# A hybrid attention and state-space block: the mixer's TensorE order written out, loads moved ahead of two stages, and a tail with its residual tiles loaded ahead

## The chip, the cores and the metric

The kernel runs on one core of one Trainium2 chip. The time is the device time of one execution in microseconds (us). Of the kernel before, three runs took 2443.05, 2445.43 and 2448.56 us; the median is 2445.43. A core has TensorE (PE in the profile; PEld is its weight load), VectorE (DVE), ScalarE (ACT), GpSimd (POOL) and SyncE (SP), whose queue here starts nearly all DMA transfers. Instructions on one engine run in order; engines wait for each other by semaphores.

## The reference

One layer on x of 1024 positions by 1024 channels, cut here to what the change touches:

```python
h = rmsnorm(x, pre_norm_mix) * (1.0 + scale_m) + shift_m
proj = h @ w_in          # q_lat, kv_lat, k_idx, w_idx, z, xbc, dt_raw, g_a, g_b
y_a = sparse_mla_attention(...) @ w_o_attn
y_b = ssd_mixer(z, xbc, dt_raw, ...) @ w_o_ssd
mix = (sigmoid(g_a) * y_a + sigmoid(g_b) * y_b) @ w_out
x = x + gate_m * rmsnorm(mix, post_norm_mix)
h2 = rmsnorm(x, pre_norm_ffn) * (1.0 + scale_f) + shift_f
u_gate, u_up = split(h2 @ w_ffn_in, 2)
f = (silu(u_gate) * u_up) @ w_ffn_out
x = x + gate_f * rmsnorm(f, post_norm_ffn)
```

`ssd_mixer` is a Mamba-2 scan: 32 heads in 8 groups, a state carried from chunk to chunk, y = (C Bᵀ · decay) X inside a chunk plus C · state from the chunks before, then `rmsnorm(y * silu(z), ssd_norm)`. All is float32.

## The kernel before, in words

Activations lie with channels on the 128 partitions and positions along the free axis, in two halves of 512 positions (b = 0, 1). A float32 product is made of three matmuls in the fp32r format: each operand is split into a high part (ACT copy) and the rest (subtraction on DVE or POOL), and hi·hi, hi·lo and lo·hi are added in PSUM. Weights come through the stream `W`: SP loads a piece of 4 tiles (`wraw`), ACT makes `whi` (L147), POOL `wlo` (L148); two pieces are ahead of the one in use. TensorE then runs 12 matmuls on a piece for one half.

Stages in order of time: input norm and projections; attention; the **mixer**; the **merge**; the second sub-layer (`early`, `gate_up`, L1324); its output product (`pfo`, L1456) with the **tail**.

*Mixer* (about 1135 to 1490 us). 32 slices of the scan, one per chunk of 256 positions and group, group by group. A slice is `ssd_in` (loads; `pcb` = C Bᵀ, L1027; transposes `px`, L1038, and `pbn`, L1047; the decay masks M on ACT and DVE) and then, one slice later, `ssd_out` (`pyd` = M X, L1071 and L1072; the state's update `pst`, L1078; `pyo` = C · state, L1083; the sum, the gate z, and a store to `d_y`). Beside them runs a filler, `beside`: 8 column tiles of g_b (`pw`), then 8 of y_a = attention output @ w_o_attn (`poa`), each in steps of 6 matmuls. Between these two lies the loading and splitting of the attention output (`atl`, 16 tiles of 128x512). `weave` alternates the steps of `ssd_in`, `ssd_out` and the filler, but this only gives priorities: the instruction order of every engine, TensorE too, comes from a scheduler that simulates the program and picks what is ready. In other stages `in_order` ties TensorE to the program's order.

*Merge*. `y_load` brings the scan's output from `d_y` (`yl`), ACT makes `yh` (L1166) and DVE `yw` (L1167): 16 slices k of 128 channels for one half. `merge` multiplies them by w_o_ssd (`pos`, 48 matmuls for a column tile), `mixed` by w_out (`pot`). In the kernel before, `y_load(0, range(16))` stands behind the whole mixer in program order.

*Tail*. For the last column tile of half 1 the product is made in two pieces of 256 positions; `outputs` multiplies the scaled tile `fv` by the spread norm `prn` (DVE, L1474), adds the residual `x1l` that SP loads from `d_x1` there and then (L1473, L1475), and stores it (L1476).

Buffers: H (32 tiles of 128x512), Q (26), R (8 of 128x1024), EV (9 of 128x512 for passing data), 5 PSUM banks for the slices. A tile waits until a buffer of its kind is free.

## Time and profile before

| | us |
|---|---|
| median of three runs | 2445.43 |
| profiled execution | 2446.71, its span 2444.9 |
| TensorE busy | 2374.4 (97% of the span) |
| DVE, ACT, POOL busy | 1434.9, 1225.8, 1081.3 |
| mean granted TensorE clock | 0.985 |

"Granted clock" is the share of full speed at which TensorE may run; 0.50 is half. A stretch of time is given by its start and end in us from the span's start; what TensorE lost in it is the stretch less its busy time, and, where the clock is below 1.00, the stretch times the missing share.

### The profile page before, as it was taken

The numbers are of one execution on the slowest core, as the hardware profiler recorded it, in microseconds if no ns is written. First come the engines' busy times: TensorE is split into PE (matmuls) and PEld (weight loads), VectorE is DVE, ScalarE is ACT, GpSimd is POOL, SyncE is SP. The second block draws the span as 40 slices with busy tenths as digits, with TensorE's granted clock in tenths as the row PEclk, the third lists the DMA queues.
The fourth block names the chain that finished last, engine by engine and source line by source line (L and its number), as shares of the span: only waits on it lengthen the run. The fifth ranks groups of instructions, "written<-read, shape, count | busy, mean of one in ns | idle before, by whom it ended". The sixth has DMA issues, their size and how long they took to land.

```text
span 2444.9 us, 34790 instructions
## 1 busy us (share of the span) xinstructions
PE 2374.4 (97%) x11940; PEld 1938.1 (79%) x11940; DVE 1434.9 (59%) x2848; ACT 1225.8 (50%) x2351; POOL 1081.3 (44%) x877
## 2 busy tenths in 40 slices
PE   7999999999999999999999999999999999999997
PEld 5788888888888788887777767888777888888886
DVE  4566776599656666665567675456476666542211
ACT  4346665567446555556666564544453222344432
POOL 2731112222235545442345435557576545544564
PEclk8999999999999999999999999999999999999998
DMA  7224212522223232234768784655564544354453
GB/s 270 91 87 127 70 64 79 164 91 100 87 63 100 91 101 85 90 97 149 222 215 266 224 275 140 223 188 165 163 213 162 160 155 150 113 167 152 137 164 112
DMA packets 219745, 352.79 MB, mean 144 GB/s; under 512 B 22016, under 2 KB 86192, under 8 KB 219568
## 3 DMA queue, kind: packets, MB, share of 16 engines
q1 hardware_dynamic: 218848, 349.99, 44.3%
q8 instruction: 94, 1.54, 0.3%
q14 instruction: 83, 0.68, 0.1%
q10 hardware_dynamic: 720, 0.58, 0.1%
HBM read 266.31 MB, written 87.32 MB: 145 GB/s over the span
## 4 chain that ended last, share of the span: by engine, by line
PE 60%; DVE 4%; DMA 3%; ACT 2%; issue 2%; POOL 2%; SPq 0%; DVEq 0%; POOLq 0%; ACTq 0%
PE p L1324 14%; PE pfo L1456 9%; PE pw L232 8%; PE pos L222 5%; PE plg L774 4%; PE poa L232 3%; PE pot L222 3%; PE po L823 2%; PE pt L807 2%; PE puq L222 2%; PE pyd L1071 1%; PE pst L1078 1%; DMA a<-w_ffn_in 1%; PE pcb L1027 1%; PE pyo L1083 1%
## 5 line engine op out<-in xcount | busy, mean ns | idle before, releaser
L148 POOL TENSOR_TENSOR wlo<-wraw,whi 128x512 fp32r<-128x512 f32 x242 | 329.3, 1363 | 531.9 <-ACT whi L147 463.9
L1324 PE MATMUL p<-xh,wr 128*128 128x512 f32 x880 | 275.4, 392 | 3.7 <-DVE g L1374 3.7
L147 ACT ACTIVATE whi<-wraw 128x512 fp32r<-128x512 f32 x242 | 151.1, 627 | 207.7 <-issue 42.3
L1456 PE MATMUL pfo<-a,fwh 128*128 128x512 f32 (+1 forms) x684 | 208.7, 386 | 1.2 <-DVE a L243 1.2
L1318 POOL TENSOR_TENSOR wr<-a,wr 128x512 fp32r<-128x512 f32 x110 | 152.9, 1403 | 101.8 <-ACT wr L1317 65.9
L1324 PEld LDWEIGHTS p<-xh,wr 128*128 128x128 f32 x880 | 166.6, 189 | 39.0 <-DVE g L1374 4.1
L1324 PE MATMUL p<-xl,wr 128*128 128x512 f32 x440 | 172.2, 391 | 0.0
L243 POOL TENSOR_TENSOR fwl<-fw,fwh 128x512 fp32r<-128x512 f32 x92 | 113.9, 1241 | 116.0 <-ACT fwh L242 109.0
L1456 PEld LDWEIGHTS pfo<-a,fwh 128*128 128x128 f32 x684 | 127.5, 188 | 28.2 <-DVE a L243 2.6
L786 ACT ACTIVATE lg<-lg,mx 128x256 f32<-128x256 f32 (+7 forms) x128 | 98.9, 773 | 70.1 <-DVE mx L783 69.1
L1456 PE MATMUL pfo<-a,fwl 128*128 128x512 f32 (+1 forms) x342 | 131.9, 386 | 0.0
L1317 ACT ACTIVATE wr<-a 128x512 fp32r<-128x512 f32 x110 | 67.9, 629 | 123.9 <-PE p L1324 95.3
L313 POOL TENSOR_TENSOR adaw<-adaw,cs 128x512 f32<-128x512 f32 x64 | 66.7, 1044 | 133.4 <-DMA adaw<-ada_w 99.0
L242 ACT ACTIVATE fwh<-fw 128x512 fp32r<-128x512 f32 x92 | 54.5, 594 | 124.7 <-PE pfo L1456 102.8
L1324 PE MATMUL p<-h2h,wr 128*128 128x512 f32 x352 | 112.4, 396 | 0.0
L634 ACT ACTIVATE junk<-acc,cand__2203 128x1024 bf16<-128x1024 f32 (+2 forms) x96 | 86.2, 898 | 44.9 <-DVE cand__2203 L677 29.0
L222 PE MATMUL pos<-yw,whi 128*128 128x512 f32 x256 | 103.0, 402 | 4.8 <-DVE yw L1167 4.8
L222 PE MATMUL pos<-yh,whi 128*128 128x512 f32 x256 | 101.5, 397 | 3.9 <-ACT yh L1166 2.3
L222 PE MATMUL pos<-yh,wlo 128*128 128x512 f32 x256 | 102.1, 400 | 0.9 <-POOL wlo L148 0.9
L585 DVE SCALAR_TENSOR_TENSOR acc<-rel,widx,acc 128x384 f32<-128x384 f32 (+2 forms) x90 | 87.1, 987 | 25.0 <-ACT rel L580 24.8
L580 ACT ACTIVATE rel<-prel 128x512 f32<-128x512 f32 (+3 forms) x160 | 77.1, 523 | 48.7 <-PE prel L579 45.2
L1324 PEld LDWEIGHTS p<-xl,wr 128*128 128x128 f32 x440 | 83.3, 189 | 17.3
(572 smaller groups left out, 6864.0 us busy)
## 6 DMA issues: line engine op xcount, KB each, us to landing
wraw<-w_in SPq DMA_DIRECT2D x130, 256.0 KB, 2.9
a<-w_ffn_in SPq DMA_DIRECT2D x124, 256.0 KB, 3.3
fw<-w_ffn_out SPq DMA_DIRECT2D x80, 256.0 KB, 2.7
adaw<-ada_w SPq DMA_DIRECT2D x64, 256.0 KB, 3.0
al<-d_ac SPq DMA_DIRECT2D x32, 512.0 KB, 5.5
wraw<-w_o_ssd SPq DMA_DIRECT2D x64, 256.0 KB, 3.3
al<-d_a SPq DMA_DIRECT2D x44, 256.0 KB, 5.3
d_a<-g SPq DMA_DIRECT2D x40, 256.0 KB, 2.4
```

The source lines that it names most:

```text
L147: behind(S.activation(hi[:, :kt], raw[:, :kt], AF.Copy))
L148: behind(G.tensor_tensor(lo[:, :kt], raw[:, :kt], f(hi[:, :kt]), op=OP.subtract))
L222: T.matmul(o, wt[:, k0 + i, :], xs[k][xi][b][:, sl], start=pi == 0 and i == 0 and wt is hi and xi == 0, stop=pi == len(pcs) - 1 and i == l ...
L232: T.matmul(o, wt[:, k0 + j, :], xs[k][xi][b], start=i == 0, stop=i == 23)
L243: (lo_eng or V).tensor_tensor(lo, src, f(hi), op=OP.subtract)
L585: V.scalar_tensor_tensor(acc[i][:, 0:n], rel[:, 0:n], ws, acc[i][:, 0:n], op0=OP.mult, op1=OP.add)
L634: S.activation(jk, y, AF.Sign, scale=-1.0, bias=a_, accum_out=o)
L774: T.matmul(p[:, 0:w2], st[qi], KVT[ki][:, o_:o_ + w2], start=x == 0, stop=x == 2)
L786: S.activation(lg[:, 0:n], lg[:, 0:n], AF.Exp, scale=-1.0, bias=m, accum_out=rr[:, 2 * t + hh:2 * t + hh + 1])
L1318: G.tensor_tensor(w[:, 1], src, f(w[:, 0]), op=OP.subtract)
L1324: T.matmul(p, w[:, wi, i], X[x][i][xi], start=start and i == 0 and k == 0, stop=i == 3 and k == 2, skip_group_check=True)
L1456: T.matmul(p, w[wi][:, k - k0], xs[k][xi][:, sl], start=k == 0 and i == 0, stop=k == FT - 1 and i == 2)
```

## The change

Five things change. (1) The mixer's TensorE instructions are tied to the program's order, and the loop is written out: all four steps of `ssd_in`, then three of `ssd_out` (its `yield` between the two halves of `pyd` is gone), with 4 or 3 filler steps spread between them, by turns. (2) Four of the attention output's tiles of half 0 are loaded into Q before the last g_b tile; the others follow it. (3) The y_a tiles 0 to 4 are made for both halves, tiles 5 to 7 first for half 0 and then for half 1, with their weights loaded a second time. (4) `y_load(0, range(12))` stands before those last three tiles of half 1, in H and Q; the four other slices stay where they were. (5) In the second sub-layer's output the residual tiles of a whole half are loaded ahead into Q; the norm of the first 256 positions is applied after 8 of the 22 k-tiles instead of 12, and its additions go to DVE and POOL by turns.

```diff
@@ ssd_out
-            if j == 0:
-                yield
@@ beside
         for t in range(8):
+            if t == 7:
+                at_load(0, range(AT_IN_Q), Q)
             yield from gate_steps(57 + t, d_gb[t])
+        at_load(0, range(AT_IN_Q, KT), H_)
+        at_load(1, range(KT), H_)
+        for ts, bs in [((t,), BS) for t in range(POA_BOTH)] + [(range(POA_BOTH, 8), (b,)) for b in BS]:
+            for t in ts:
+                W.plan(col_tile(a["w_o_attn"][t]))
+                w = wpieces(ks8)
+                for b in bs:
...
+            if bs == (0,):
+                y_load(0, range(12), y_place)
@@ mixer
-    if True:
+    with in_order(mybir.EngineType.PE):
         prev = None
-        for s_ in [(c, g) for g in range(GROUPS) for c in range(NCH)] + [None]:
+        for n, s_ in enumerate([(c, g) for g in range(GROUPS) for c in range(NCH)] + [None]):
             z = {}
-            weave(ssd_in(*s_, z) if s_ else iter(()), 4 if s_ else 0, ssd_out(*prev) if prev else iter(()), 4 if prev else 0, filler, 4)
+            steps = ([ssd_in(*s_, z)] * 4 if s_ else []) + ([ssd_out(*prev)] * 3 if prev else [])
+            k, nf = 0, 4 - n % 2
+            for _ in range(0 if s_ else 4):
+                next(filler, None)
+            for i, g in enumerate(steps):
+                next(g)
+                while k < nf and k * len(steps) < nf * (i + 1):
+                    next(filler, None)
+                    k += 1
@@ merge
-    y_load(0, range(16), H_)
+    y_load(0, range(12, 16), y_place)
@@ tail
-    def outputs(b, c0, cn, fv, r, end):
+    def x1_load(b, where):
+        xs = [where("x1l") for t in range(8)]
+        for t in range(8):
+            SP.dma_start(xs[t], d_x1[t][:, half(b)])
+        return xs
+    def outputs(b, c0, cn, fv, xs, r, share, end):
...
-            xr, f_ = EV("x1l")[:, 0:cn], fv[t][:, c0:c0 + cn]
-            SP.dma_start(xr, d_x1[t][:, cl])
+            xr, f_ = xs[t][:, c0:c0 + cn], fv[t][:, c0:c0 + cn]
             V.tensor_tensor(f_, f_, prf, op=OP.mult)
-            (V if t % 2 and end else G).tensor_tensor(xr, xr, f_, op=OP.add)
+            (V if t % 2 and share else G).tensor_tensor(xr, xr, f_, op=OP.add)
...
-                if c.start and k0 == 8:
-                    outputs(1, 0, 256, fv[1], r, False)
+                if c.start and k0 == 4:
+                    outputs(1, 0, 256, fv[1], x1_, r, True, False)
```

**A slice on TensorE.** First before the change, then with it, around the ninth `pcb`; `pw` is the filler.

```order
L1071 MATMUL pyd<-al,X 64x256
L1072 MATMUL pyd<-M,X 64x128
L1027 MATMUL pcb<-ld 128x256
L1028 MATMUL pcb<-ld 128x128
L1071 MATMUL pyd<-al,X 64x256
L1072 MATMUL pyd<-M,X 64x128
...
L1038 MATMUL px<-ident,ld 128x128 x4
L1083 MATMUL pyo<-ld,state 128x256 x2
L1047 MATMUL pbn<-ident,ld 128x128 x2
L232 MATMUL pw<-h6h,wlo 128x512
```

```order
L1030 MATMUL pcb<-ld 128x256
L1031 MATMUL pcb<-ld 128x128
L235 MATMUL pw<-h2h,whi 128x512
...
L1041 MATMUL px<-ident,ld 128x128 x4
L1050 MATMUL pbn<-ident,ld 128x128 x2
L235 MATMUL pw<-h4h,whi 128x512
...
L1074 MATMUL pyd<-al,X 64x256
L1075 MATMUL pyd<-M,X 64x128
...
L1084 MATMUL pyo<-ld,state 128x256 x2
```

Before, the two halves of `pyd` stood around the next slice's `pcb` in 31 slices, and nearly all of a slice's matmuls followed each other. Now `pcb`, `px` with `pbn`, and `pyd` with what follows it stand apart, with six filler matmuls between them, and all eight rows of `pyd` follow each other.

**SP's queue where the scan's output is loaded.** Before, then with the change; `wraw` is the weight stream, `al`, `zy` and `ld` belong to slices, `d_ya` and `d_y` are stores.

```order
L1164 DMA yl<-d_y 128x512
L1129 DMA d_ya<-ya 128x512
L1093 DMA d_y<-zy 128x2x256
L1062 DMA zy<-d_z 128x2x256
L1164 DMA yl<-d_y 128x512 x6
L1010 DMA ld<-d_bc 128x2x256
L1011 DMA ld<-d_xs 128x2x256
```

```order
L1149 DMA d_ya<-ya 128x512
L1117 DMA yl<-d_y 128x512 x9
L149 DMA wraw<-w_o_ssd 128x512 x2
L1117 DMA yl<-d_y 128x512 x2
L149 DMA wraw<-w_o_ssd 128x512
L1149 DMA d_ya<-ya 128x512
L1094 DMA d_y<-zy 128x2x256
L149 DMA wraw<-w_o_ssd 128x512
L1149 DMA d_ya<-ya 128x512
L149 DMA wraw<-w_o_ssd 128x512 x2
L1117 DMA yl<-d_y 128x512 x2
```

Before, the loads lay among those of the last three slices. Now the first twelve are queued behind the last slice's loads, beside 72 `poa` matmuls of half 1 that stand on TensorE between the last `pyd` and the first `pos`; the last four come behind six weight pieces.

**SP's queue in the tail**, from the residual loads of the last 256 positions on. Before, then with the change, where the queue's last row of transfers follows the last weights.

```order
L1473 DMA x1l<-d_x_109 128x256 x8
L1476 DMA out<-x1l 128x256 x4
L1473 DMA x1l<-d_x_109 128x256
L1476 DMA out<-x1l 128x256 x2
L1473 DMA x1l<-d_x_109 128x256
L1476 DMA out<-x1l 128x256 x2
L1473 DMA x1l<-d_x_109 128x256 x4
```

```order
L1462 DMA fw<-w_ffn_out 128x512 x5
L1462 DMA fw<-w_ffn_out 128x256
L1504 DMA out<-x1l 128x256 x12
```

No load is left between the stores.

## The prediction, written before the changed kernel was run

> **What bounds the kernel now.** I read the page's busy times first, then TensorE's waits in the mixer and merge, then the same stretch by windows, and then timelines of single places.

> ```profile
> span 2444.9 us, 34790 instructions
> PE 2374.4 (97%) x11940; PEld 1938.1 (79%) x11940; DVE 1434.9 (59%) x2848; ACT 1225.8 (50%) x2351; POOL 1081.3 (44%) x877
> ```

> TensorE is busy but for 70.5 us. A change that moves work on the other engines can win only parts of those, time at a low clock, or time in which TensorE is "busy" without streaming. The waits of TensorE from 1130 to 1560 us:

> ```profile
> PE pos L222 <- DVE yw L1167: 4.8, 4, 1.7
> PE pos L222 <- ACT yh L1166: 2.3, 2, 1.5
> PE poa L232 <- ACT ath L242: 2.2, 1, 2.2
> PE pyd L1071 <- DVE al L1032: 0.8, 1, 0.8
> ```

> The starts of the two stages whose operands come from DRAM (`poa`, `pos`) make nearly all of it; in 32 slices only one waited for its own operands, 0.8 us. By windows (stretch, its length, PE busy, then PEld, DVE, ACT, POOL; clock, DMA share, GB/s):

> ```profile
> 1135.00:1280.30 145.30, 145.30 (x792) 113.35 (x791) 81.22 (x130) 89.53 (x200) 55.28 (x45) 1.00 0.66 208
> 1280.30:1300.00 19.70, 15.94 (x79) 10.91 (x79) 13.18 (x20) 12.86 (x29) 11.17 (x10) 0.83 0.95 322
> 1300.00:1440.00 140.00, 140.00 (x756) 109.31 (x756) 99.11 (x148) 80.16 (x177) 61.00 (x48) 1.00 0.71 227
> 1440.00:1493.00 53.00, 45.83 (x238) 33.71 (x235) 43.22 (x63) 37.22 (x76) 22.87 (x17) 0.90 0.68 234
> 1493.00:1530.00 37.00, 34.25 (x148) 27.03 (x147) 12.75 (x18) 13.51 (x24) 24.31 (x19) 0.95 0.51 169
> ```

> Between the starts TensorE is idle for nothing at full clock. At the attention output's start (row 2) it loses 19.70 - 15.94 = 3.8 us idle and 19.70 x 0.17 = 3.3 us by clock: 7.1. At the merge's (rows 4 and 5) 7.2 + 2.8 us idle and 53 x 0.10 + 37 x 0.05 = 7.1 by clock: 17.1, of which I count 15, since some low clock falls on idle time. So a stall costs nearly twice its length.

> [...]

> **The change part by part.** *One block of `pyd` instead of two.* A slice with `pcb` between the halves of `pyd`, a slice without (the last), a lone `pcb`, and a `pbn` between filler matmuls:

> ```profile
> 1476.83 0.66 PE L1071 MATMUL pyd<-al,X 128*64 128x256 f32 x4
> ...
> 1479.30 1.13 PE L1078 MATMUL pst<-Xd,bn 128*128 128x256 f32 x4
> 1480.26 0.60 PE L1038 MATMUL px<-ident,ld 128*128 128x128 f32 x4
> 1480.70 1.03 PE L1083 MATMUL pyo<-ld,state 128*128 128x256 f32 x4
> ...
> 1488.19 0.39 PE L222 MATMUL pos<-yh,wlo 128*128 128x512 f32 x1
> 1488.51 0.66 PE L1071 MATMUL pyd<-al,X 128*64 128x256 f32 x4
> ...
> 1490.01 1.13 PE L1083 MATMUL pyo<-ld,state 128*128 128x256 f32 x4
> ```

> ```profile
> 1135.06 0.68 PE L1027 MATMUL pcb<-ld 128*128 128x256 f32 x2
> ...
> 1136.02 0.39 PE L232 MATMUL pw<-h4l,whi 128*128 128x512 f32 x1
> ...
> 1160.76 0.40 PE L232 MATMUL pw<-h2l,whi 128*128 128x512 f32 x1
> 1161.00 0.38 PE L1047 MATMUL pbn<-ident,ld 128*128 128x128 f32 x2
> ...
> 1161.45 0.40 PE L232 MATMUL pw<-h3h,whi 128*128 128x512 f32 x1
> ```

> Starts count, since matmuls overlap. The sandwich takes 1479.30 - 1476.83 = 2.47 us; `pyd` in one block 1490.01 - 1488.51 = 1.50; the lone `pcb` 1136.02 - 1135.06 less one filler matmul of 0.23 = 0.73. That saves 2.47 - 1.50 - 0.73 = 0.24 us in each of 31 slices, 7.4 us. Against it, a slice now leaves the filler more often, up to three times more. Entering `pyd` costs 1488.51 - 1488.19 = 0.32 instead of 0.23, 0.09 more; if every new break cost that, 31 x 3 x 0.09 = 8.4 us would be lost, net -1. The `pbn` row says otherwise: 1161.45 - 1161.00 less 0.23 leaves 0.22 us for two transposes, and four `px` in an unbroken block took 0.44 (1480.26 to 1480.70), so that break was free. I take **-6** us, bounds -7.4 and +1.

> *Attention output loaded earlier.* Four tiles of half 0 get into Q while g_b still runs, so 12 `poa` matmuls are ready when it ends; the others need H buffers that the last g_b tile gives back, half 0's first. In the order of SP these loads stand ahead of the next but one slice's `ld`, `al` and `zy`: eight in a row, so a late one delays a slice's operands. Before the fifth tile is needed, TensorE now has those 12 matmuls (2.8 us), a `pcb`, `px`, `pbn`, `pyd` and the state's matmuls, about 4.5 us by the rows above: 7 us. A load's issue, landing, ACT and DVE fit into that, with little to spare. Of 6.5 to 7.1 us I leave 1.5 as new waits: **-5**, bounds -7 and -2.

> *The scan's output loaded earlier.* What it needs, by rows of 1440 to 1480 us:

> ```profile
> L1167 DVE SCALAR_TENSOR_TENSOR yw<-yl,vec,yh 128x512 fp32r<-128x512 f32 x14 | 13.3, 971 | 0.8 <-ACT yh L1166 0.7
> L1166 ACT ACTIVATE yh<-yl,vec 128x512 fp32r<-128x512 f32 x14 | 9.7, 714 | 1.5 <-DMA yl<-d_y 1.5
> 1450.00:1453.00 3.00, 3.00 (x14) 1.64 (x13) 2.53 (x5) 3.00 (x9) 0.00 (x0) 0.59 1.05 379
> yl<-d_y SPq DMA_DIRECT2D x32, 256.0 KB, 5.6
> ```

> Twelve slices take 12 x 0.262 MB / 379 GB/s = 8.3 us of transfers, 12 x 0.71 = 8.6 us of ACT and 12 x 0.97 = 11.7 us of DVE. The 72 `poa` matmuls between the last `pyd` and the first `pos` last 72 x 0.23 = 16.6 us: covered. Before, DVE had this beside the last three slices' own work. ACT's queue now holds a `whi` behind every second to fourth `yh`, and TensorE uses a weight piece up in 12 x 0.23 = 2.8 us, so a late `yl` holds up the weights; the second load of w_o_attn's tiles 5 to 7 adds six pieces. The last four slices are late next: SP issues them behind weight pieces that wait for TensorE, about when `pos` starts; 36 matmuls, 8.3 us, stand before them, against 5.6 us to landing, 0.7 and four times 0.97. That is short by 1 to 2 us, and a clock drop may come with it. I take **-12** of 15; bounds -17 and -6.

> *The tail.*

> ```profile
> 2423.42 0.16 DVE L259 TENSOR_SCALAR v<-p 128x2 f32<-128x2 f32 x1 [0.88 <-PE p L256]
> 2432.28 0.16 DVE L259 TENSOR_SCALAR v<-p 128x2 f32<-128x2 f32 x1 [0.70 <-PE p L256]
> 2432.80 0.70 POOL L261 TENSOR_TENSOR r<-v,nhalf 128x2 f32<-128x2 f32 x1
> 2434.28 2.73 DVE L1474 TENSOR_TENSOR fv<-fv,prn 128x256 f32<-128x256 f32 x8 [1.85 <-PE prn L267]
> 2434.84 0.73 POOL L1475 TENSOR_TENSOR x1l<-x1l,fv 128x256 f32<-128x256 f32 x1 [1.33 <-DMA out<-x1l]
> 2436.94 1.86 DVE L1475 TENSOR_TENSOR x1l<-x1l,fv 128x256 f32<-128x256 f32 x3
> 2441.49 0.42 DVE L1475 TENSOR_TENSOR x1l<-x1l,fv 128x256 f32<-128x256 f32 x1 [2.69 <-DMA x1l<-d_x]
> ```

> The last addition waits for its residual until 2441.49, and the span ends 2444.9 - 2441.91 = 3.0 us after it. With the residuals there, DVE alone sets the end: 2.73 us for eight products and four additions at 1.86 / 3 = 0.62, 5.2 us from 2434.28, so 2439.5 instead of 2441.9: 2.4 us. With additions at 0.42, 3.2; if the stores queue up instead, 1. Then `r` is no longer behind POOL's additions: 2432.80 - 2432.44 = 0.36 us, 0.3 of it saved. The norm's `r` is ready in time for its earlier place. **-2.7**, bounds -3.5 and -1.

> [...]

> *The written order itself.* Any instruction on TensorE that is late now holds up the filler behind it, and that holds up the PSUM banks that DVE and ACT drain. The nearest row is one wait of 0.8 us in 32 slices. Loads for a slice still stand about two slices ahead of its `pcb` on SP. I take **+2**; bounds 0 and +8.

> **The sum.** -6 - 5 - 12 - 2.7 + 2 = -23.7 us. The profiled execution took 2446.71 us, 1.8 outside its span, and stood 1.3 above the median of 2445.43. 2446.7 - 23.7 = 2423.0 for a profiled execution, and with the same 1.3 off, **2422 us** for a median. Taking the bounds that are likely together, the forecast's own range is 2411 to 2434.

> **The rivals.**

> *The stall only moves.* Sixteen tiles need the same transfers, ACT and DVE as before; at the merge DMA was at a share of 1.05. If the earlier loads starve slices, or the weights behind `yh`, half of both stage terms (8.5 us) stays: 2422 + 8.5 = 2430.5. For it: SP's one queue and the short margin of the last four. Against: 16.6 us of cover with no slice in it.

> *The written order stalls every slice.* If `pyd`, or a bank that DVE has not yet drained, is late by 0.8 us in each of 31 slices, that is 24.8 us instead of 2, and the time is 2445; with 1.2 us, 37, or 2457. From 0.8 us on it cancels everything. Against it: DVE is busy 99.11 of 140 us there, and a slice's products have most of the next slice's time. For it: TensorE no longer takes what is ready.

> *The clock does not come back.* If the drops of the clock have another cause than these stalls, the two stages give back idle time alone, 3.8 + 7.2 + 2.8 less the same 4.5 left as new waits, 9.3 instead of 17: 2430. The three rows whose clock is below 1.00 are those with idle time, so I give it little. [...]

> *It does not do what it says.* The order view shows that TensorE's and SP's instructions move as told, but if the merge's start is bound by something unseen, only 6 + 2.7 remain: 2439.

> **How the numbers follow.** Forecast 0.62; moved stall 0.17; slices stall 0.12 (three quarters of it slower or the same); clock 0.05; little done 0.04. Changes within 0.2%, 4.9 us, can hardly be told from none: between 2440.5 and 2450.3 lie some 4 in 100, mostly of the stalling slices; slower 7; faster 89. The range reaches from the forecast's lower end over the moved stall: 2409 to 2438.

> **What would show it.** In the changed profile `pyd` to `pyo` or `pst` in 1.50 us everywhere; clock 1.00 and idle under 2 us around the first `poa` and the first `pos`; no TensorE wait for `al`, `M` or a slice's `ld` above 1 us; no residual load after the last matmul, and the last addition about 5 us after the last `prn`. It is wrong if waits appear on `pyd`, `pcb` or `pyo` in many slices, if `pos` waits for `yw` of the last four slices for more than 3 us, or if TensorE's first rows after the mixer run at half clock.

## The result, and the profile after

The changed kernel takes **2430.97 us** (median of four executions, 2427.84 to 2434.19), the kernel before 2445.2 (four, 2443.05 to 2448.56). The ratio is 0.9941, its 95% interval 0.9922 to 0.9959: faster by 14 us, where 2422 and so 24 us were predicted. The time lies inside the range of 2409 to 2438, close to what one rival gave, "the stall only moves" (2430.5). The profiled execution is the longest of the four, 2434.19 us. Its page begins:

```profile
span 2432.4 us, 34774 instructions
PE 2363.3 (97%) x11940; PEld 1939.3 (80%) x11940; DVE 1440.5 (59%) x2852; ACT 1227.6 (50%) x2357; POOL 1092.3 (45%) x879
```

TensorE is busy 11.1 us less; 69.1 us of the span are still idle, against 70.5. TensorE's waits from 1130 to 1560 us, with the change (total, times, longest):

```profile
PE pyd L1074 <- DVE al L1035: 3.9, 4, 1.4
PE pbn L1050 <- ACT bn L1052: 2.5, 1, 2.5
PE poa L235 <- ACT ath L245: 2.0, 2, 1.8
PE poa L235 <- DVE atl L246: 1.9, 2, 1.7
PE pos L225 <- POOL wlo L151: 1.3, 2, 0.6
PE px L1041 <- DVE zy L1087: 0.6, 1, 0.6
```

The waits of `pos` for `yh` and `yw`, 7.1 us before, are gone. In their place stand waits inside slices (`pyd`, `pbn`, `px`) and at `poa`. Of the four in the first row, 1.42 us at 1217.7 and 1.14 us at 1381.3 lie in slices far from both starts. By windows, the attention output's start and the merge's start, first of the kernel before, then with the change; the two last rows are the stretches that the changed kernel spent at half clock there:

```profile
1285.00:1330.00 45.00, 42.06 (x207) 31.65 (x206) 37.98 (x50) 31.79 (x70) 27.42 (x20) 0.92 0.88 284
...
1440.00:1545.00 105.00, 95.08 (x451) 73.16 (x448) 61.43 (x87) 57.82 (x110) 55.52 (x42) 0.93 0.59 198
```

```profile
1285.00:1330.00 45.00, 35.81 (x162) 25.65 (x161) 29.22 (x40) 28.20 (x61) 23.92 (x17) 0.81 0.84 274
...
1440.00:1545.00 105.00, 102.94 (x470) 83.77 (x469) 48.41 (x62) 47.79 (x78) 61.25 (x46) 1.00 0.63 204
...
1293.10:1299.90 6.80, 4.76 (x19) 2.63 (x20) 6.77 (x9) 5.51 (x15) 5.84 (x4) 0.50 0.72 173
1313.60:1323.80 10.20, 7.69 (x18) 4.99 (x19) 8.53 (x11) 7.46 (x13) 8.69 (x6) 0.50 1.06 370
```

One start got better and the other worse. For a sum that counts nothing twice I take a stretch's length less TensorE's busy time (idle), and half of the busy time in its half-clock stretches (clock); what is left is work at full speed. At the attention output that is 45.00 - 35.81 = 9.2 idle and (4.76 + 7.69) / 2 = 6.2 by clock, **15.4 us**; before, 2.9 and 3.1, 6.0. At the merge it is 2.1 and 0, **2.1 us**; before, 9.9 and 5.8, 15.8. From the first `pcb` to the first `pot`, in us:

| kernel | ratio to before, 95% | first `pcb` to first `pot` | idle in other slices | attention output, 1285 to 1330 | merge, 1440 to 1545 | rest |
|---|---|---|---|---|---|---|
| before | 1 | 433.3 | 0.8 | 6.0 | 15.8 | 410.8 |
| the change | 0.9941 (0.9922 to 0.9959) | 424.3 | 2.6 | 15.4 | 2.1 | 404.2 |
| the change, second trace | 0.9937 (0.9918 to 0.9956) | 426.0 | 2.0 | 13.6 | 6.3 | 404.1 |
| order alone | 1.0004 (0.9991 to 1.0017) | 431.2 | 3.1 | 18.1 | 7.9 | 402.0 |
| attention loads late | 0.9963 (0.9949 to 0.9976) | 431.8 | 4.7 | 19.8 | 3.5 | 403.9 |
| scan loads late | 0.9964 (0.9952 to 0.9977) | 430.5 | 2.4 | 16.6 | 8.4 | 403.2 |
| order not tied | 0.9956 (0.9940 to 0.9973) | 423.4 | 0.6 | 11.9 | 9.4 | 401.5 |
| first four spread | 0.9974 (0.9961 to 0.9987) | no trace to read | | | | |
| last twelve spread | 0.9939 (0.9921 to 0.9958) | 426.7 | 4.9 | 16.1 | 2.2 | 403.4 |
| all spread | 0.9931 (0.9913 to 0.9950) | 420.2 | 8.1 | 8.1 | 1.4 | 402.7 |
| loads ahead, splits tied | 0.9957 (0.9942 to 0.9972) | 427.0 | 8.3 | 10.8 | 2.8 | 405.1 |
| nine buffers | 0.9928 (0.9913 to 0.9943) | 421.2 | 2.9 | 10.0 | 4.4 | 403.9 |
| nine buffers, all spread | 0.9922 (0.9909 to 0.9935) | 419.6 | 2.0 | 10.0 | 4.7 | 402.9 |
| one source for the splits | 0.9934 (0.9918 to 0.9950) | 421.5 | 2.0 | 11.5 | 3.7 | 404.2 |

Each row of the five last columns is one execution's trace, each figure rounded by itself. Executions of one kernel on one chip lie up to 15 us apart (order alone: 2440.21 to 2454.74), and both traces of the change show the longest execution of their series, so a difference of a few us between two rows is not shown by them alone. The one profile of "first four spread" fell on a slow execution, 7839.98 us at a mean granted clock of 0.368, which is left out of its time and ratio too.

How the attention output's start is lost, in the changed kernel's timelines (start, duration, engine and line; in brackets the idle time before, and who ended it). TensorE, then ACT, then SP's queue:

```profile
1293.56 0.69 PE L1050 MATMUL pbn<-ident,ld 128*128 128x128 f32 x2 [2.53 <-ACT bn L1052]
...
1295.27 1.11 PE L1074 MATMUL pyd<-al,X 128*64 128x256 f32 x2 [1.02 <-DVE al L1035]
...
1303.29 0.39 PE L235 MATMUL pw<-h7h,wlo 128*128 128x512 f32 x1
...
1312.98 0.50 PE L235 MATMUL poa<-ath,whi 128*128 128x512 f32 x1 [1.80 <-ACT ath L245]
...
1319.78 0.80 PE L235 MATMUL poa<-atl,whi 128*128 128x512 f32 x1 [1.69 <-DVE atl L246]
```

```profile
1286.98 0.63 ACT L245 ACTIVATE ath<-atl 128x512 fp32r<-128x512 f32 x1 [2.30 <-DMA atl<-d_att]
1287.52 1.69 ACT L1025 ACTIVATE al<-al,acum 128x256 f32<-128x256 f32 x4
...
1292.62 0.62 ACT L245 ACTIVATE ath<-atl 128x512 fp32r<-128x512 f32 x1
1293.14 0.36 ACT L1052 ACTIVATE bn<-pbn 128x256 f32<-128x256 f32 x1
```

```profile
1302.68 0.37 SPq L1065 DMA_DIRECT2D zy<-d_z  x1
...
1306.04 0.43 SPq L1131 DMA_DIRECT2D atl<-d_att  x1
```

Two groups of waits. Before the first `poa`, the four early tiles' splits stand in ACT's queue between a slice's masks: one waits 2.30 us for its transfer with `al` behind it, another has `bn` behind it, and `pbn`, `al` and so `pyd` are late. After it, the fifth tile is late: the last g_b matmul (`pw`) starts at 1303.29, but SP issues `atl` at 1306.04, because a slice's `zy` load ahead of it waited until 1302.68 for a buffer. From that issue to the end of its `ath` it takes 6.9 us (1312.93), about what the 12 `poa` matmuls and the slice cover.

The tail, in the kernel before and then with the change, from the last squares on:

```profile
2430.26 0.38 ACT L1462 ACTIVATE sqm<-pfo 128x256 f32<-128x256 f32 x1 [7.88 <-PE pfo L1456]
...
2430.68 0.90 DVE L1465 TENSOR_TENSOR sqm<-sqm 128x256 f32<-128x256 f32 x1 [1.33 <-ACT sqm L1462]
```

```profile
2421.32 0.38 ACT L1484 ACTIVATE sqm<-pfo 128x256 f32<-128x256 f32 x1 [7.83 <-PE pfo L1478]
...
2421.74 0.43 DVE L1487 TENSOR_TENSOR sqm<-sqm 128x256 f32<-128x256 f32 x1 [0.84 <-ACT sqm L1484]
...
2423.86 0.43 PE L270 MATMUL prn<-ident,r 128*128 128x128 f32 x2 [1.04 <-POOL r L264]
2424.33 2.74 DVE L1502 TENSOR_TENSOR fv<-fv,prn 128x256 f32<-128x256 f32 x8 [1.31 <-PE prn L270]
...
2426.99 1.90 DVE L1503 TENSOR_TENSOR x1l<-x1l,fv 128x256 f32<-128x256 f32 x4
```

From these squares to the end it was 2444.9 - 2430.26 = 14.64 us and is 2432.4 - 2421.32 = 11.08: 3.6 us won. The last addition ends 2428.89 - 2424.33 = 4.6 us after the first product with the last `prn` starts; before, that was 2441.91 - 2434.28 = 7.6.

### The profile page after: what moved, and what is told of

Read it like the earlier page. It is cut to its first block, busy times and chain, and to the rows that moved or that the text cites. A ratio compares the mean times of both kernels' runs of the same rounds, so it can differ in the third digit from the quotient of the medians.

```text
span 2432.4 us, 34774 instructions
## 1 busy us (share of the span) xinstructions
PE 2363.3 (97%) x11940; PEld 1939.3 (80%) x11940; DVE 1440.5 (59%) x2852; ACT 1227.6 (50%) x2357; POOL 1092.3 (45%) x879
## 4 chain that ended last, share of the span: by engine, by line
PE 54%; DVE 5%; DMA 4%; ACT 3%; issue 3%; POOL 2%; SPq 1%; DVEq 0%; POOLq 0%; ACTq 0%
PE p L1346 13%; PE pfo L1478 9%; PE pw L235 7%; PE pos L225 6%; PE plg L777 4%; PE pot L225 3%; PE po L826 2%; PE pt L810 2%; PE poa L235 2%; PE puq L225 2%; DMA d_y<-zy 1%; POOL wr L1340 1%; PE pyd L1074 1%; DMA zy<-d_ea 1%; PE pst L1079 1%
## 5 line engine op out<-in xcount | busy, mean ns | idle before, releaser
L151 POOL TENSOR_TENSOR wlo<-wraw,whi 128x512 fp32r<-128x512 f32 x248 | 341.1, 1377 | 527.3 <-ACT whi L150 455.5
L588 DVE SCALAR_TENSOR_TENSOR acc<-rel,widx,acc 128x384 f32<-128x384 f32 (+2 forms) x90 | 87.1, 988 | 24.8 <-ACT rel L583 24.7
## 6 DMA issues: line engine op xcount, KB each, us to landing
wraw<-w_in SPq DMA_DIRECT2D x130, 256.0 KB, 2.9
a<-w_ffn_in SPq DMA_DIRECT2D x124, 256.0 KB, 3.4
fw<-w_ffn_out SPq DMA_DIRECT2D x80, 256.0 KB, 2.7
adaw<-ada_w SPq DMA_DIRECT2D x64, 256.0 KB, 3.0
wraw<-w_o_ssd SPq DMA_DIRECT2D x64, 256.0 KB, 3.2
al<-d_a SPq DMA_DIRECT2D x44, 256.0 KB, 5.4
d_a<-g SPq DMA_DIRECT2D x40, 256.0 KB, 2.3
```

The costliest lines, as they stand in the source:

```text
L151: behind(G.tensor_tensor(lo[:, :kt], raw[:, :kt], f(hi[:, :kt]), op=OP.subtract))
L588: V.scalar_tensor_tensor(acc[i][:, 0:n], rel[:, 0:n], ws, acc[i][:, 0:n], op0=OP.mult, op1=OP.add)
```

## The experiments

In the expectations "the queues" is the theory that splits waiting in ACT's, DVE's and SP's queues make slices late; "the fixed order" and "the transfers" are its first rivals.

**Attention loads late**, part 2 undone.

```diff
-AT_IN_Q = 4
+AT_IN_Q = 0
```

> The changed kernel with no tile of the attention output loaded early: all 16 follow the last g_b tile, as before the change. In the profile of the change TensorE lost 17.7 us around the attention output's start: 0.65 + 2.53 + 1.02 + 0.56 = 4.8 idle in slices before the first poa and 4.4 idle after it, and 6.8 and 10.2 us at half clock, 3.4 and 5.1. Theory, the queues: the splits of the early tiles stand in ACT's and DVE's queues ahead of a slice's masks and wait there for their transfers. Then the waits on al, bn and M before the first poa go, with their half clock, and a start like that of the kernel before stays, 7 to 9 us in all: 2431 - 9 to 11 = 2420 to 2422. Rival, the fixed order: TensorE can no longer pass a late slice, whatever is loaded when; then the waits before the first poa stay and all 16 loads are waited for besides, 2431 to 2438. Rival, the transfers: the DMA share there is 0.8 to 0.95 and the same bytes must come in any case; then 2429 to 2433.

Measured: 0.9963, 2438.14 us. The waits before the first `poa` did shrink, but one wait of 15.6 us for the first `ath` took the place of all others there, and the start lost 19.8 us. So the early loads do help, by 19.8 - 15.4 = 4.4 us there (6.2 by the second trace), about the size of the predicted -5. What the theory missed is that the starting point was no longer the 6 us of the kernel before. The rival of the fixed order had it that all 16 loads would be waited for, and its 2431 to 2438 came closest, though the waits before the first `poa` did not stay as it said.

**First four spread**, one tile before each of the g_b tiles 4 to 7.

```diff
-            if t == 7:
-                at_load(0, range(AT_IN_Q), Q)
+            if t > 3:
+                at_load(0, range(t - 4, t - 3), Q)
```

> The changed kernel with its four early tiles spread, one before each of the g_b tiles 4 to 7 instead of four before tile 7. Theory, the queues: with one split for a slice instead of four no slice's masks are late, and the waits before the first poa go with their half clock (4.8 + 3.4 = 8.2 us); those after it (4.4 + 5.1) stay: 2423, 2421 to 2425. Rival, the fixed order: a slice is late by another cause, 2430 to 2432. Rival, the transfers: the four tiles are gone from the busy stretch, 1 MB or 2.6 us at 400 GB/s, 2428 to 2430.

Measured: 0.9974, 2440.18 us (median of nine), slower than every theory said. Without a trace to read, why it is slower than the change stays open.

**Last twelve spread.**

```diff
-            yield from gate_steps(57 + t, d_gb[t])
-        at_load(0, range(AT_IN_Q, KT), H_)
-        at_load(1, range(KT), H_)
+            for i, _ in enumerate(gate_steps(57 + t, d_gb[t])):
+                if t == 7 and i > 3:
+                    at_load(0, range(AT_IN_Q + i - 4, AT_IN_Q + i - 3), H_)
+                yield
...
-                    yield from dense_steps(p, b, w, AT)
+                    for i, _ in enumerate(dense_steps(p, b, w, AT)):
+                        if t == b == 0:
+                            at_load(1, range(3 * i, min(3 * i + 3, KT)), H_)
+                        yield
```

> The changed kernel with its four early tiles as they are, but the other four of half 0 loaded one by one during the second half of the last g_b tile, when half 0 has already given back its buffers, and the eight of half 1 three at a time in the first y_a tile's steps. Theory, the queues: SP issued those twelve in a row at 1306 to 1316 us, behind a zy load that blocked it until 1302.7; issued earlier and spread, the waits after the first poa go with their half clock (4.4 + 5.1 = 9.5), and those before it stay or grow by the four further splits in that place, 1 to 3 us: 2423 to 2426. Rival, the fixed order: 2430 to 2432. Rival, the transfers: the same bytes in the same 40 us, 2429 to 2432.

Measured: 0.9939, 2432.14 us; the interval holds the change's own ratio. All waits of `poa` are gone, as the theory has it, but 7.9 us of `pbn` for `cbm`, 6.1 of `pyd` for `al` and 2.8 of `px` came instead. The longest is one split's: ACT waited 5.79 us for the transfer of a tile that SP had issued at 1292.98, DVE 5.66 us for ACT's part of it, and the slice's `cbm` stood behind it on DVE (1298.67). So the earlier loads' splits cost what the loads gave.

**All spread**, both edits together.

```diff
+            if t > 3:
+                at_load(0, range(t - 4, t - 3), Q)
+            for i, _ in enumerate(gate_steps(57 + t, d_gb[t])):
+                if t == 7 and i > 3:
+                    at_load(0, range(AT_IN_Q + i - 4, AT_IN_Q + i - 3), H_)
+                yield
...
+                        if t == b == 0:
+                            at_load(1, range(3 * i, min(3 * i + 3, KT)), H_)
```

> Both spreads together. Theory, the queues: both groups of waits go, 17.7 less some 2 left over, 2431 - 15 = 2416, 2414 to 2419, and the profile shows clock 1.00 from 1285 to 1330 us. Rival, the fixed order: 2429 to 2432. Rival, the transfers: at least the 10.5 us that 4.2 MB take at 400 GB/s compete with the slices' own, so half of it stays, 2422 to 2426.

Measured: 0.9931, 2430.55 us. The start's loss fell to 8.1 us, but that in other slices rose from 2.6 to 8.1. Two of its waits on TensorE, and ACT before the first of them:

```profile
1248.05 0.66 PE L1074 MATMUL pyd<-al,X 128*64 128x256 f32 x4 [1.85 <-DVE al L1035]
...
1258.40 0.66 PE L1074 MATMUL pyd<-al,X 128*64 128x256 f32 x4 [2.25 <-DVE al L1035]
```

```profile
1220.60 0.63 ACT L245 ACTIVATE ath<-atl 128x512 fp32r<-128x512 f32 x1 [3.31 <-DMA atl<-d_att]
...
1242.45 0.63 ACT L245 ACTIVATE ath<-atl 128x512 fp32r<-128x512 f32 x1 [1.82 <-DMA atl<-d_att]
1242.99 1.70 ACT L1025 ACTIVATE al<-al,acum 128x256 f32<-128x256 f32 x4
```

Two splits whose transfers are late by 3.31 and 1.82 us hold up `al`, which stands behind each of them in ACT's queue. The first shows in no wait of TensorE, but it uses up the slices' slack: `al` ends 4.9, 5.0 and 5.2 us before the `pyd` at 1227.04, 1235.69 and 1245.96 of the changed kernel, and 0.6, 0.9 and 0.06 us before the same three here. The second then comes out as 1.85 us of idle TensorE. So a late split delays slices by way of the queues, and the delay is carried from slice to slice.

That is not so of every wait for `al`. The wait at 1258.40 has no split on ACT, DVE or POOL in the 10 us before it; there DVE's `al` runs beside POOL's `wlo`, and takes longer than the 1.22 us before the wait at 1248.05:

```profile
1255.46 1.71 POOL L151 TENSOR_TENSOR wlo<-wraw,whi 128x512 fp32r<-128x512 f32 x1
...
1255.97 2.29 DVE L1035 TENSOR_TENSOR al<-al,cbm 128x1024 f32<-128x1024 f32 x1
```

Part of that wait is thus the longer `al` beside POOL, 2.29 us against 1.22 (the last section), and part may be the delay carried over. And one more, 1.42 us at 1217.85, stands at the same slice in all eleven traces with the tied order, in order alone too, where the first split comes at 1306.85: it belongs to the loop. The mechanism of the queues is shown; that spreading would remove its cost is not.

**Order alone**: the kernel before with part 1.

```diff
-    if True:
+    with in_order(mybir.EngineType.PE):
...
+            steps = ([ssd_in(*s_, z)] * 4 if s_ else []) + ([ssd_out(*prev)] * 3 if prev else [])
...
-            if j == 0:
-                yield
```

> The kernel before with part 1 alone: TensorE's instructions tied to the written order, pyd in one block; loads and tail as before. By the prediction's own terms, -6 + 2: 2441 against 2445 for the kernel before. Theory, the join: the run with all 16 attention tiles after the last g_b tile had one wait of 15.6 us at the first poa, and with its half clock lost some 27 us from 1285 to 1325 us where the kernel before lost 7; a fixed order cannot fill that time with slices. Then the sum is -7.5 for pyd and the breaks, +2.5 for waits in slices, +20 at the attention output, and 0 to +5 at the merge: 2460 to 2465, slower than before by 0.6 to 0.8 per cent.

Measured: 1.0004, 2445.78 us: no difference that can be told, neither the 4 us of the prediction's terms nor the 15 to 20 us loss expected here. The trace shows two large changes of opposite sign: the attention output's start lost 18.1 instead of 6.0 us, the merge's 7.9 instead of 15.8. At the attention output, first the kernel before (TensorE and SP, around the last `pw`), then order alone:

```profile
1279.96 0.39 PE L232 MATMUL pw<-h7h,wlo 128*128 128x512 f32 x1
...
1280.46 0.90 SPq L1119 DMA_DIRECT2D atl<-d_att  x2
...
1285.90 0.38 PE L1047 MATMUL pbn<-ident,ld 128*128 128x128 f32 x2
```

```profile
1293.15 0.59 PE L1027 MATMUL pcb<-ld 128*128 128x256 f32 x2
...
1307.53 0.80 PE L232 MATMUL poa<-ath,whi 128*128 128x512 f32 x1 [13.57 <-ACT ath L242]
```

```profile
1295.67 0.37 SPq L1062 DMA_DIRECT2D zy<-d_z  x1
...
1299.51 0.90 SPq L1117 DMA_DIRECT2D atl<-d_att  x2
```

Before, SP issued the first `atl` 0.5 us after the last `pw` started, and TensorE filled some 5 us with a whole slice's matmuls. In the written order only a `pcb` stands between, and `atl` comes 6.4 us after that, behind a load that waited until 1295.67 for a buffer and the issues that follow it. At the merge the opposite: y_a steps dealt out evenly leave TensorE `poa` matmuls until 1464.1 us, long after the last `pyd` at 1446.5, while the last slices settle.

**Scan loads late**, parts 3 and 4 undone.

```diff
-POA_BOTH = 5
+POA_BOTH = 8
...
-            if bs == (0,):
-                y_load(0, range(12), y_place)
...
-    y_load(0, range(12, 16), y_place)
+    y_load(0, range(16), lambda k: H_)
```

> The changed kernel without parts 3 and 4: the y_a tiles in their old order and all 16 slices of the scan's output loaded behind the mixer. The starts of pos cost 17 us before and 2 now. By the traces, 2431 + 14.7 = 2446; by the prediction's term, 2431 + 12 = 2443. If the fixed order makes TensorE stand through the whole first load (store of y, load, ACT, DVE, some 10 to 15 us) as it does at the attention output, 2451 to 2458. If the term is overestimated because other work would have hidden it, under 2440.

Measured: 0.9964, 2437.26 us. The merge's start loses 8.4 us, not 17: the written order alone had taken about half away, and the early loads took the other 6.3 (2.1 by the second trace). "Other work would have hidden it" is what happened.

**Order not tied**: the same loop, and TensorE's order left to the scheduler.

```diff
-    with in_order(mybir.EngineType.PE):
+    if True:
```

> The changed kernel with TensorE's tie to the written order taken off; the loop is written the same way, and the scheduler picks TensorE's order. Theory, the fixed order is what turns a late slice into a stall: most of the 9.2 us idle and 8.5 us by clock at the attention output goes, 2418 to 2424, with pyd perhaps in pieces again (+0 to +6). Theory, the queues alone: the scheduler's order is as fixed on the chip as the written one, made for the times it simulates, so the waits stay: 2429 to 2435.

Measured: 0.9956, 2434.24 us, as the queues alone have it; the interval holds the change's ratio. The stretch is 423.4 against 424.3 and 426.0. The attention output loses 11.9 and the merge 9.4: again one start against the other. By this trace it is the loop as written, more than the tie, that makes the loss at the attention output.

**Loads ahead, splits tied.** The loads are told apart from the splits, and a split stands behind the masks of the slice in work.

```diff
+            if t == 6:
+                at_load(0, range(4))
+            for i, _ in enumerate(gate_steps(57 + t, d_gb[t])):
+                if t == 7:
+                    if i < 4:
+                        at_split(0, (i,), Q)
+                    if i == 4:
+                        at_load(0, range(4, 8))
+                    if i == 7:
+                        at_split(0, range(4, 8), H_)
+                yield
...
+                after_masks(S.activation(hi, raw[b, k], AF.Copy))
+                after_masks((G if k % 2 else V).tensor_tensor(lo, raw[b, k], f(hi), op=OP.subtract))
```

> The changed kernel with the attention output's loads apart from their splits: tiles 0 to 3 are loaded one g_b tile ahead of their splits, 4 to 7 when half 0 has given back its buffers, half 1 when the first y_a tile starts; and each split is tied behind the masks of the slice in work on ACT and on its own engine (before, ACT's order had splits between a slice's masks). Theory, the queues: no mask waits behind a split that waits for a transfer; 17.7 us fall to 3 to 6: 2417 to 2420, clock above 0.95 from 1285 to 1325 us. Rival, the splits' own time on ACT and DVE (16 x 0.55 and 8 x 0.65 us) is too much for a slice: the waits move to pyd and stay, 2427 to 2432. Rival, the transfers: 2425 to 2430.

Measured: 0.9957, 2436.21 us; no gain, and 4 us above the highest figure of any theory. The start loses 10.8 us, other slices 8.3, 5.4 of it from 1330 to 1440: 3.4 us there is one `pbn` at 1330.5, right behind the last splits, which start until 1323.9. The waits moved and stayed, as the first rival, the splits' own time, has it; but 3.2 us of `pcb` waits for `ld` belong to SP's queue, so neither cause is excluded.

**Nine buffers** for the slices, with two fewer for passing data, on the change and on all spread. SP's own waits in the changed kernel from 1140 to 1280 us are what they are aimed at:

```profile
SPq L1065 <- DMA d_y<-zy: 30.8, 6, 6.6
SPq L1013 <- DMA d_y<-zy: 23.1, 6, 5.3
```

```diff
-    n_slots = dict(H=32, Q=26, R=8, EV=9, raw=4, hi=3, lo=3)
+    n_slots = dict(H=32, Q=26, R=9, EV=7, raw=4, hi=3, lo=3)
```

> The changed kernel with nine buffers of 128x1024 for the slices instead of eight, and seven for passing data instead of nine, to make room. In the trace of the change SP waits 12 times in 14 slices, 54 us in all and up to 6.6 at a time, for a store of y to give back such a buffer before it can issue the next slice's loads; everything behind (atl too) waits with it, and a slice's masks end 0.3 us before their pyd. Theory, slices without slack: a ninth buffer lets the loads start about a third of a slice (3 us) sooner; the 4.8 us of waits before the first poa fall to 1 or 2 and their half clock goes, and those after it fall by the 2 to 3 us that atl is issued earlier: 2431 - 8 to 11 = 2420 to 2423. Rival, ACT's and DVE's own order (splits between masks) is enough by itself: no change, 2429 to 2433. With seven passing buffers too few elsewhere: above 2435.

> The same nine buffers in the kernel whose sixteen attention loads are spread over slices. There seven waits of pyd for al, 0.6 to 2.5 us and 12.7 in all, were left, nearly one for each slice that had a split to do. Theory, slices without slack: most of these go; from the first pcb to the first pot 420.3 falls to 408 to 413, and the time is 2417 to 2421. Rival, ACT's and DVE's own order: 2428 to 2432, and the same waits for al.

Measured: 0.9928, 2428.04 us, and 0.9922, 2426.36 us, the shortest measured here; the change beside them on the same chip stood at 0.9937. Against the kernel before both are faster beyond their intervals; against the change the intervals overlap. The start loses 10.0 us in both; on the change, the time was expected to fall by 8 to 11 us. A gain from the buffer is therefore not shown. The edit also did only part of what it was for: in its trace on the change SP still waits 24.0 us at `ld` and 16.4 at `al` for `d_y<-zy`, 40.4 where the rows above add up to 53.9.

**The change again**, nothing edited.

> The changed kernel itself once more, for a second trace of it beside the others on one chip. If the loss at the attention output belongs to the order of the queues, it shows again: idle near 9 us and some 17 us at half clock from 1285 to 1330 us, 422 to 426 us from the first pcb to the first pot. If it was one execution's chance (its time was the longest of four), idle under 5 us and a stretch below 418.

Measured: 0.9937, 2431.72 us, the start's loss 13.6 us in a stretch of 426.0: it belongs to the kernel, not to one execution. The merge's 2.1 in the first trace was the better of two.

**One source for the splits.**

```diff
+        one = EV("atl")
+        SP.dma_start(one, d_att[0][:, half(0)])
...
-                t = EV("atl")
-                SP.dma_start(t, d_att[k][:, half(b)])
-                AT[k][0][b], AT[k][1][b] = split(where, t, "at", lo_eng=G if k % 2 else V)
+                AT[k][0][b], AT[k][1][b] = split(where, one, "at", lo_eng=G if k % 2 else V)
```

> The changed kernel with 15 of the 16 attention loads left out: one tile is loaded when the mixer starts, and all sixteen splits read it (so y_a is made of that tile alone). Splits, buffers and TensorE's order stay; what goes is SP's issues, 4 MB of transfers and every wait of a split for its landing. In two traces of the change the stretch from 1285 to 1330 us lost 15.4 and 13.6 us. Theory, waiting for transfers (behind SP's blocked queue, and in ACT's queue ahead of masks): 10 or more of it go, 2418 to 2421. Rival, the splits' own time on ACT and DVE, 16 x 0.55 and 8 x 0.65 us in the queues ahead of the masks: half or more stays, 7 us and over, 2424 to 2432.

Measured: 0.9934, 2428.57 us; the start still loses 11.5 us. This kernel leaves out what the other fifteen tiles hold, so its output is not the layer's, and only its time is of use. Without their transfers, 2 to 4 of 13.6 to 15.4 us go: by these three traces the rival holds. But the waits are not the same ones: those of `poa` are gone, and `pbn` waits 3.3 us for `cbm` instead. Its window of the start:

```profile
1285.00:1308.00 23.00, 15.20 (x61) 10.54 (x60) 21.05 (x24) 16.22 (x35) 17.46 (x11) 0.78 0.52 168
```

DVE is busy 21.05 of 23.00 us: here DVE, not TensorE, sets the pace. All sixteen splits start between 1277.8 and 1302.0 us, and DVE's part of them stands among its masks. This trace does not tell how much of the loss with transfers is the same DVE time: from 1285 to 1330 us the changed kernel's DVE is busy 29.22 of 45.

## Why the prediction was right and wrong

By its own steps, from the first trace (second in brackets):

- *One block of `pyd`*, -6, bounds -7.4 and +1: right, as far as the column "rest" can tell, which holds more than this. The rest fell by 410.8 - 404.2 = 6.6 us (6.7), and `pyd` to `pst` or `pyo` takes 1.50 us in 30 of the 32 slices (before, in one). The bound +1 counted three new breaks in every slice; in every second slice `pcb` and `px` still follow each other, so there are fewer.

```profile
1307.68 0.66 PE L1074 MATMUL pyd<-al,X 128*64 128x256 f32 x4
...
1309.18 1.13 PE L1079 MATMUL pst<-Xd,bn 128*128 128x256 f32 x4
```

- *The written order*, +2: right for the slices elsewhere, 2.6 - 0.8 = 1.8 us (1.2). In the first trace the 2.6 are the two waits of `pyd` for `al`, 1.42 and 1.14 us, that order alone has too. But its larger effects were not in the step at all: +12.1 us at the attention output and -7.8 at the merge when it is made alone. The prediction took each start's loss in the old order as the amount that loads could win, though the same change also rewrote which matmuls stand around the starts.
- *Attention output loaded earlier*, -5: **the step that failed**. Measured from before to after, 15.4 - 6.0 = +9.4 us (+7.6). Two sentences of it broke. "Of 6.5 to 7.1 us I leave 1.5 as new waits" had the wrong start: in the written order there were 18 to 20 us to win, and the early loads won 2.7 to 6.2 of them. "A load's issue, landing, ACT and DVE fit into that" gave the price of one tile and not that of its place in the queues: SP's, blocked until 1302.7 us, and ACT's and DVE's, where the splits hold up a slice's masks. The step named the danger ("a late one delays a slice's operands") for SP alone.
- *Scan's output loaded earlier*, -12: right in size, -13.7 us (-9.5), the clock at 1.00 in the first trace. But the size is partly luck: the step counted the loads alone, and by the runs with order alone and with late scan loads the loads gave 6.3 us (2.1) of it, the order the rest.
- *The tail*, -2.7, bounds -3.5 and -1: -3.6 us, just outside. The products and additions take 4.6 us where the step had 5.2. What additions on both engines cost each other is not shown by this: POOL's four stand beside DVE's products, not its additions. The part before `prn` became shorter by 0.8 us instead of 0.3, since DVE's `sqm` takes 0.43 us where it took 0.90 beside POOL's additions, and `r` no longer waits for those.

Added up, -6.6 + 1.8 + 9.4 - 13.7 - 3.6 = -12.7 us, and the span fell by 12.5. The 11 us between this and the predicted 23.7 are the attention output's, which is 14.4 off its term, less 3.4 that the other steps gave beyond theirs. So the time lies inside the range, and inside the forecast's own 2411 to 2434, by the width of the bounds, not because the sum was right. The prediction's own signs told it: waits for `al` above 1 us (1.42), and idle of 9.2 us and half clock around the first `poa`.

The rival *the stall only moves* had the time, 2430.5, and for the attention output its mechanism, "if the earlier loads starve slices"; at the merge, where it put 6 of its 8.5 us, the first trace shows nothing of the kind. In the second there is one such wait, by its "weights behind `yh`": `whi` stands behind two `yh` that waited for `yl` until 1475.0, `pos` waits 1.77 us for it, and a step at half clock follows. *The clock does not come back* had 2430 too, by a cause that did not occur: at the merge of the first trace the clock came back with the idle time. *The written order stalls every slice* is excluded: 1.8 us in the slices elsewhere.

What stays open: how the loss at the attention output divides between late transfers, the splits' own time and what DVE and POOL lose beside each other; why the first four tiles spread alone are slower than the change, and why the rest differs by up to 3.6 us between kernels with the same matmuls (401.5 to 405.1).

## What to carry to other kernels

A stall is worth what it costs in the order that the change itself makes: when an order is rewritten and loads are moved in one edit, first ask which matmuls will stand around each start, and price the loads against that. Work that is put on ACT and DVE "beside" a steady loop has a place in their queues, and may wait there for its own transfer (in all spread 3.31 and 1.82 us): it first uses up the slack of the loop's operands (here some 5 us of `al` before `pyd`), and what comes late after that is idle time on TensorE. So read that slack from the trace before spreading loads over a loop. A buffer more for the loads that pace it (2428.0 against 2431.7 us, within overlapping intervals) may help; here it is not shown to.

## What the runs showed of the hardware

```profile
1289.70:1293.11 3.41, 1.33 (x6) 0.75 (x4) 1.03 (x3) 3.41 (x7) 2.83 (x3) 1.00 0.99 373
```

```profile
1256.95:1260.36 3.41, 1.96 (x18) 1.67 (x19) 3.38 (x5) 3.41 (x10) 1.18 (x2) 1.00 0.93 226
1308.19:1311.60 3.41, 1.24 (x13) 0.94 (x14) 3.38 (x5) 3.01 (x9) 1.65 (x2) 0.99 0.83 202
```

The first has 2.08 us idle, and half clock follows. The second has 1.45 idle, since its wait of 2.25 us began a step earlier, and no drop follows; the third holds a wait of 2.17 us whole, and one does. In the kernel before and in the change, from 37 us on (what comes before is the kernel's beginning), and in the other eleven traces from 40 to 350, 655 to 965, 1269 to 1569 and 1884 to 2183 us, the least idle time in a step at full clock with a drop behind it is 1.18 us (the change, at 1637.86), and the most without one 1.80 (loads ahead, splits tied, at 1325.51).

*DVE and POOL took longer beside each other.* One source for the splits, DVE's and POOL's timeline, and below two of the same instructions in the changed kernel, where they overlap for 0.15 us:

```profile
1295.09 1.23 DVE L1035 TENSOR_TENSOR al<-al,cbm 128x1024 f32<-128x1024 f32 x1
1295.19 2.26 POOL L151 TENSOR_TENSOR wlo<-wraw,whi 128x512 fp32r<-128x512 f32 x1
...
1296.24 1.75 DVE L1035 TENSOR_TENSOR M<-M,cbm 128x512 f32<-128x512 f32 x1
```

```profile
1277.56 0.68 DVE L1035 TENSOR_TENSOR M<-M,cbm 128x512 f32<-128x512 f32 x1
...
1278.09 1.31 POOL L151 TENSOR_TENSOR wlo<-wraw,whi 128x512 fp32r<-128x512 f32 x1 [0.40 <-ACT whi L150]
```

`M` takes 1.75 us where it took 0.68, and `wlo` 2.26 where it took 1.31. `wlo` starts at 1295.19 while `al` runs until 1296.32; with its own 1.31 behind that it would end at 1297.63, and it ends at 1297.45. `M` then would end 0.68 after it, at 1298.13, and ends at 1297.99. So an estimate from these times by which each starts only when the other has ended comes within 0.18 us of both ends; the cause is not shown. In the same trace a mask of DVE (`M` at 1302.19) beside one of the splits takes 1.75 us too, and eight of the sixteen splits are POOL's.
